# A causal zero block kept in tiles, the last outputs in pairs, and a swish written in token order by ScalarE

## The chip, the cores and the metric

The kernel runs on one core of a Trainium2 chip. A core has five engines that run beside each other and meet through semaphores: TensorE (matmuls; the profile calls it PE, and its weight loads PEld), VectorE (DVE), ScalarE (ACT), GpSimd (POOL) and SyncE (SP), which here issues DMAs. Matmuls write to PSUM, eight banks of 128 partitions by 512 floats; all else lives in SBUF or, between stages, in DRAM. The metric is the time of one execution on the device in microseconds; less is better. All data is float32. Where a matmul's operand is to be exact, it is split into a rounded part `hi` (type float32r) and a rest `lo`, and three products (hi·hi, hi·lo, lo·hi) replace one.

## The reference, cut to what matters

One layer of a decoder: `SEQ` 1024 tokens, `D_MODEL` 1024 channels. A mixing sub-layer runs a convolution branch and an attention branch on the same input; a SwiGLU sub-layer follows.

```
def hybrid_mixer(h, ...):
    proj = h @ w_in
    glu_in, qkv, gates = split(proj)
    u = u_val * sigmoid(u_gate)
    u = causal_depthwise_conv(u, conv_w, conv_b)          # 31 taps, 512 channels
    u = silu(layernorm(u, conv_ln_g, conv_ln_b))
    y_conv = u @ w_conv_out
    o = stick_breaking_attention(q, k, v)                 # 8 heads of 64
    y_att = o @ w_att_out
    merged = sigmoid(g_conv) * y_conv + sigmoid(g_att) * y_att
    return merged @ w_o

# stick-breaking attention, for each block of queries; causal means key < query
z = q k^T / 8
a = where(causal, exp(log_sigmoid(z) + sum of log_sigmoid(-z) over the later keys), 0)
o = a @ v

x = x + ga1 * rmsnorm(hybrid_mixer(h))
x = x + ga2 * rmsnorm((silu(gate) * up) @ w_ffn_out)      # gate, up = split(h2 @ w_ffn_in)
```

## The kernel before, in words

Channels lie on partitions and tokens in the free dimension, except in attention, where the scores have queries on partitions. Two mechanisms set the order of instructions. Most of the kernel is written in plain program order and is ordered by a planner (`TileContext(nc, schedule_with_timeline_sim=True)`): it takes what is ready on a simulated timeline, by priority; priority is the place in the program, and `tc.high_priority(offset=...)` moves a block forward. The engines' queues are then fixed, and each runs its own strictly in that order. Some stretches are ordered by hand: `pin(start)` (line 186) chains all instructions issued since `start` on TensorE, VectorE and ScalarE. A buffer is a tile of a pool with a `tag` and a number of `bufs`; a new tile of that tag waits for the readers of the one whose place it takes.

**Attention** (lines 522 to 598, function `head`, called eight times under high priority). For each pair of query blocks `c` (256 queries, four pairs in all; the order of the pairs is in `CORDER`) and each half of up to 512 keys, `z` comes from two matmuls (lines 551, 552) and, on the diagonal, a third that adds the mask (554). ScalarE takes two sigmoids of it (555, 556), VectorE a running product from right to left (559) and a product (561); the result `beta` has queries on partitions. For each pair of key blocks `jp`, TensorE turns four 128x128 blocks into one PSUM bank `tr` (line 571: two key blocks `jj` by two query blocks `ii`). ScalarE copies the bank to `ahi` (574), VectorE subtracts to get `alo` (575), both 128x512 with two buffers in turn, and four matmuls with the values add to `av` (580, 581). Where `jp == c`, the block with the later keys and the earlier queries is zero by causality; there the transpose reads the constant tile `zeros`. A head has ten such banks, four of them on the diagonal: 80 and 32 in all. The matmuls of projections, values, the input gate (`glu`), the convolution (`conv`) and the merge gates are written around the heads, and the planner places them between the steps of attention.

**The convolution's normalisation and swish** (`ln_all`, lines 724 to 762). The convolution works with tokens split by their remainder modulo eight (`PH = 8`), so its output `cacc[ct]` lies as eight runs of 128: `(r m)`, remainder first. The normalisation keeps that order. Then, for each of four channel tiles of 128x1024, ScalarE writes the sigmoid of the scaled input to `csig` (756) and the scaled input over itself (757); VectorE multiplies the two and writes to `csil` in token order `(m r)` (760), that is, with a step of eight floats between successive elements. `split_r` (718) makes `chi` and `clo` of it, which are the operands of the convolution branch's projection (`y_conv`, 774). `ln_all` is issued with `LN_PRI` ahead of the rest of the merge gates' last five products (`other_five`, 689), which use ScalarE and VectorE for their own splits (`w_op`, 399).

**The end** (lines 1673 to 1709). The last projection is done by quarters (a Strassen-Winograd scheme of seven products). The last quarter of tokens by channels, `c == 0`, runs in two halves of 256 tokens, `h = 0, 1`. In the second, the sums for the norm end on TensorE (`fsum`, 1708), `rstd_from` (150) makes the factor `rs`, and `finish` (1613) writes the outputs: for `m` of 0 to 3 and `i` of 0 to 1, a 128x256 product with `rs` (line 1626 for `m < 2`, line 1629 for the rest, which reads the result from PSUM, `last`), an addition of the residual `xr` (1631, through `add`, 1528), and a DMA of each pair to the output (1632, `load`, 103).

Of the kernel before, what the change touches and what calls it, by code (L numbers as in the profile page):

```python
# [11 lines left out]
F32R = mybir.dt.float32r  # L12
BF16 = mybir.dt.bfloat16
AF = mybir.ActivationFunctionType
# [61 lines left out]
def tile_block(ctx: ExitStack, tc: tile.TileContext, xT, vecs, ada1, ada2, win, wv, wcv, wat, wo, w1, w2, cvw, out):  # L76
# [341 lines left out]
    with ExitStack() as sC:  # L418
        pc = mkpool(sC, "pc")
        with ExitStack() as sA:  # L420
# [69 lines left out]
            def qk_pair(p):  # L490
# [28 lines left out]
                            dve.tensor_tensor(kl[i][dst, cs], b[c][src], ks[i][src, cs], op=ALU.subtract)  # L519
                return qs, ks, kl  # L520

            def head(p, hh, qst, kst, klo, vts, oT):
                half = slice(0, HD) if hh == 0 else slice(HD, P)
                other = slice(HD, P) if hh == 0 else slice(0, HD)
                hidx = (2 * p + hh) % 4
                tag = f"{p}_{hh}"
                av = None
                order = CORDER[2 * p + hh]
                for ci, c in enumerate(order):
                    if ci % 2 == 0:  # L530
                        av = psv.tile([P, CH], F32, tag="av", name=f"av{tag}_{c}")
                    avc = av[:, (c % 2) * 256:(c % 2) * 256 + 256]
                    kaps = {}
                    nsc = 1 if c < 2 else 2
                    for sc in range(nsc - 1, -1, -1):
                        probs = []
                        for i in (2 * c, 2 * c + 1):
                            W = P * (i + 1)
                            if i not in kaps:
                                kaps[i] = pa.tile([P, T], F32, tag="kap", name=f"ka{tag}_{i}", bufs=2)  # L540
                            kap = kaps[i]
                            s_lo, s_hi = sc * CH, min(W, (sc + 1) * CH)
                            w = s_hi - s_lo
                            beta = pa.tile([P, CH], F32, tag="beta", name=f"be{tag}_{i}_{sc}", bufs=4)
                            tcols = slice(i * P, (i + 1) * P)
                            z = psz.tile([P, CH], F32, tag="z", name=f"z{tag}_{i}_{sc}")
                            z_lo = s_lo if w >= 256 else max(0, s_hi - 256)
                            z_hi = max(s_hi, z_lo + 256)
                            zw, zo = z_hi - z_lo, s_lo - z_lo
                            diag = s_hi == W  # L550
                            pe.matmul(z[:, :zw], qst[:, tcols], kst[:, z_lo:z_hi], start=True, stop=False)  # L551
                            pe.matmul(z[:, :zw], qst[:, tcols], klo[:, z_lo:z_hi], start=False, stop=not diag)
                            if diag:
                                pe.matmul(z[:, zo + w - P:zo + w], identb, mask, start=False, stop=True)  # L554
                            act.activation(kap[:, s_lo:s_hi], z[:, zo:zo + w], AF.Sigmoid, bias=0.0, scale=-0.125)  # L555
                            act.activation(beta[:, :w], z[:, zo:zo + w], AF.Sigmoid, bias=0.0, scale=0.125)  # L556
                            rev = kap[:, s_lo:s_hi][:, ::-1]
                            init = 1.0 if diag else kap[:, s_hi:s_hi + 1]
                            dve.tensor_tensor_scan(rev, rev, rev, init, op0=ALU.mult, op1=ALU.bypass)  # L559
                            m = w - 1 if diag else w  # L560
                            dve.tensor_tensor(beta[:, :m], beta[:, :m], kap[:, s_lo + 1:s_lo + 1 + m], op=ALU.mult)  # L561
                            probs.append(beta)
                        for jp in range(min(c, 2 * sc + 1), 2 * sc - 1, -1):
                            tr = pst.tile([P, CH], F32, tag="tr", name=f"tr{tag}_{c}_{jp}")
                            for jj in range(2):
                                j = 2 * jp + jj
                                for ii in range(2):
                                    jo = (j - 4 * sc) * P
                                    src = zeros if (jp == c and jj == 1 and ii == 0) else probs[ii][:, jo:jo + P]
                                    o = jj * 256 + ii * P  # L570
                                    pe.transpose(tr[:, o:o + P], src, ident)  # L571
                            ahi = pa.tile([P, CH], F32R, tag="ahi", name=f"ahi{tag}_{c}_{jp}", bufs=2)
                            alo = pa.tile([P, CH], F32R, tag="alo", name=f"alo{tag}_{c}_{jp}", bufs=2)
                            act.activation(ahi, tr, AF.Copy)  # L574
                            dve.tensor_tensor(alo, tr, ahi, op=ALU.subtract)  # L575
                            for jj in range(2):
                                j = 2 * jp + jj
                                lhs = vts[j][:, hidx].rearrange("p a d -> p (a d)")
                                cols = slice(jj * 256, jj * 256 + 256)
                                pe.matmul(avc, lhs, ahi[:, cols], start=(jp == c and jj == 0), stop=False)  # L580
                                pe.matmul(avc, lhs, alo[:, cols], start=False, stop=(jp == 0 and jj == 1))  # L581
                    if ci % 2 == 1:
                        cs = slice((c // 2) * CH, (c // 2 + 1) * CH)
                        act.activation(oT[half, cs], av[other], AF.Copy)
                        dve.tensor_tensor(oT[half, cs], av[half], oT[half, cs], op=ALU.add)
# [47 lines left out]
    with ExitStack() as sG:  # L633
# [90 lines left out]
        def ln_all():  # L724
# [27 lines left out]
            for ct in range(CONVT):  # L752
                a = cacc[ct]
                g, b_ = vec[:, C_LNG + ct:C_LNG + ct + 1], vec[:, C_LNB + ct:C_LNB + ct + 1]
                sg = hp.tile([P, T], F32, tag="act", name=f"csig{ct}")
                act.activation(sg, a, AF.Sigmoid, bias=b_, scale=g)
                act.activation(a, a, AF.Identity, bias=b_, scale=g)
                o = hp.tile([P, T], F32, tag="act", name=f"csil{ct}")
                ar, sr = (t.rearrange("p (r m) -> p r m", r=PH) for t in (a, sg))
                (pool if ct in SILU_POOL else dve).tensor_tensor(  # L760
                    o.rearrange("p (m r) -> p r m", r=PH), ar, sr, op=ALU.mult)
                cacc[ct] = o

        a2 = deque(range(2 * KT, 4 * KT))
# [689 lines left out]
    with ExitStack() as sG:  # L1454
# [144 lines left out]
        def sq_tile(name):  # L1599
            return po_.tile([P, CH], F32, tag="wt", name=name, bufs=3)  # L1600
# [12 lines left out]
        def finish(c, h, ps_sum, yy, last=None):  # L1613
# [2 lines left out]
            dcols = slice(c * CH + h * n, c * CH + (h + 1) * n)  # L1616
            rs = pg.tile([P, CH], F32, tag="rs", name=f"frs{c}{h}", bufs=2)[:, :n]
            m, a = (sq_tile(f"frs{c}{h}{i}")[:, :n] for i in "ma")
            rstd_from(rs, m, a, ps_sum, D)
            for m in range(4):  # L1620
                xr = xrs[c, m]
                y = ytile[yy[m // 2], m % 2]
# [157 lines left out]
```

## Time and profile before

| | us |
|---|---|
| median of 3 runs | 1416.66 |
| lowest and highest | 1416.08, 1422.94 |
| profiled execution | 1420.87 |
| its span, first to last instruction | 1419.1 |
| TensorE busy in that span | 1389.1 |
| VectorE busy | 1061.3 |
| ScalarE busy | 650.8 |
| GpSimd busy | 96.3 |

The profile is one execution, 4.2 us above the median. Its views name an instruction by engine, line, operation and tile, with its form (partitions x elements, type); durations are in us on the timeline and in ns in groups. In the groups, the part behind the last bar is idle time of the engine just before these instructions, and what ended it. Matmuls overlap in their pipeline, so a matmul's duration is longer than the distance to the next one's start. A wait for several semaphores is put down to the one that came last.

### The profile page before, as it was taken

The numbers are of one execution on the slowest core, as the hardware profiler recorded it, in microseconds if no ns is written. First come the engines' busy times: TensorE is split into PE (matmuls) and PEld (weight loads), VectorE is DVE, ScalarE is ACT, GpSimd is POOL, SyncE is SP. The second block draws the span as 40 slices with busy tenths as digits, with TensorE's granted clock in tenths as the row PEclk, the third lists the DMA queues.
The fourth block names the chain that finished last, engine by engine and source line by source line (L and its number), as shares of the span: only waits on it lengthen the run. The fifth ranks groups of instructions, "written<-read, shape, count | busy, mean of one in ns | idle before, by whom it ended". The sixth has DMA issues, their size and how long they took to land.

```text
span 1419.1 us, 18807 instructions
## 1 busy us (share of the span) xinstructions
PE 1389.1 (98%) x6886; PEld 1161.1 (82%) x6886; DVE 1061.3 (75%) x1602; ACT 650.8 (46%) x1136; POOL 96.3 (7%) x183
## 2 busy tenths in 40 slices
PE   7999999999999999999999999999999999999996
PEld 4888898898888878888877778888888887888886
DVE  6788688666776779779589878788777776785357
ACT  5275466354553547413356543334444444433441
POOL 0000000000000101000011110001111110000000
PEclk8899999999999999999999999999999999999999
DMA  9112032122163654784934535456777769588733
GB/s 383 64 45 75 30 110 84 45 80 99 51 204 104 224 178 165 282 280 133 375 121 163 180 146 171 165 177 206 252 254 252 261 235 390 178 331 287 279 117 119
DMA packets 91116, 258.73 MB, mean 182 GB/s; under 512 B 9744, under 2 KB 20112, under 8 KB 90000
## 3 DMA queue, kind: packets, MB, share of 16 engines
q1 hardware_dynamic: 75088, 202.99, 42.0%
q0 software_dynamic: 15936, 54.54, 10.2%
q8 instruction: 54, 0.88, 0.3%
q14 instruction: 38, 0.31, 0.1%
HBM read 190.91 MB, written 66.58 MB: 181 GB/s over the span
## 4 chain that ended last, share of the span: by engine, by line
PE 87%; DVE 6%; DMA 3%; ACT 2%; issue 1%; SPq 0%; DVEq 0%; ACTq 0%; POOLq 0%
PE ka L958 12%; PE ka L1489 9%; PE kc L958 7%; PE pwo L881 6%; PE pb L1489 4%; PE pgv L180 3%; PE pg L180 3%; PE pyc L180 3%; PE pya L180 3%; PE pv L481 3%; PE pcv L461 3%; PE ka L415 2%; PE tr L571 2%; PE ke L1066 2%; PE pq L180 2%; PE pgg L180 2%
## 5 line engine op out<-in xcount | busy, mean ns | idle before, releaser
L559 DVE TENSOR_TENSOR_SCAN ka<-ka 128x128 f32<-128x128 f32 (+2 forms) x96 | 91.4, 968 | 22.8 <-ACT ka L555 22.5
L555 ACT ACTIVATE ka<-z 128x128 f32<-128x128 f32 (+2 forms) x96 | 47.1, 496 | 59.1 <-PE z L554 32.6
L575 DVE TENSOR_TENSOR alo<-tr,ahi 128x512 fp32r<-128x512 f32 x80 | 53.2, 685 | 18.2 <-ACT ahi L574 17.7
L574 ACT ACTIVATE ahi<-tr 128x512 fp32r<-128x512 f32 x80 | 46.4, 602 | 37.7 <-PE tr L571 25.9
L1489 PE MATMUL ka<-gt,w2f 128*128 128x512 f32 x264 | 63.4, 389 | 0.1
L561 DVE TENSOR_TENSOR be<-be,ka 128x127 f32<-128x127 f32 (+2 forms) x96 | 53.4, 572 | 9.7 <-ACT be L556 5.0
L1489 PEld LDWEIGHTS ka<-gt,w2f 128*128 128x128 f32 x264 | 49.5, 188 | 10.8 <-issue 0.5
L1066 PE MATMUL ke<-b,w_hi 128*128 128x512 f32 x176 | 55.1, 394 | 0.0
L135 DVE SCALAR_TENSOR_TENSOR ada<-ada,cb 128x1024 f32<-128x1024 f32 x32 | 38.8, 1223 | 19.6 <-DMA ada<-in_ada_dram 19.6
L556 ACT ACTIVATE be<-z 128x128 f32<-128x128 f32 (+2 forms) x96 | 46.2, 496 | 9.6 <-PE tr L571 9.5
L571 PE MATMUL tr<-ident,be 128*128 128x128 f32 x288 | 47.8, 273 | 0.4 <-DVE alo L575 0.4
L580 PE MATMUL av<-ahi,vst 128*128 128x256 f32 x160 | 44.2, 292 | 0.0
L461 PE MATMUL pcv<-ph,cvw 128*128 128x128 f32 x320 | 42.5, 276 | 0.9 <-DMA ph<-v_d 0.9
L581 PE MATMUL av<-alo,vst 128*128 128x256 f32 x160 | 42.8, 293 | 0.0
L461 PEld LDWEIGHTS pcv<-ph,cvw 128*128 128x128 f32 x320 | 39.5, 192 | 1.6 <-issue 1.3
L1066 PEld LDWEIGHTS ke<-b,w_hi 128*128 128x128 f32 x176 | 33.0, 188 | 7.8 <-issue 1.0
L481 PE MATMUL pv<-wv_hi,hhi 128*128 128x256 f32 x128 | 36.8, 288 | 2.1 <-DVE qst L505 1.4
L159 ACT ACTIVATE gt<-X 128x512 fp32r<-128x512 f32 x33 | 20.4, 630 | 39.1 <-PE ka L1489 12.1
L481 PE MATMUL pv<-wv_hi,hlo 128*128 128x256 f32 x128 | 36.7, 287 | 0.0
L481 PE MATMUL pv<-wv_lo,hhi 128*128 128x256 f32 x128 | 36.4, 285 | 0.0
L551 PE MATMUL z<-kst,qst 128*128 128x256 f32 (+2 forms) x96 | 36.2, 382 | 0.0
L571 PEld LDWEIGHTS tr<-ident,be 128*128 128x128 f32 x288 | 34.7, 140 | 1.8 <-PE z L554 0.5
(532 smaller groups left out, 4108.5 us busy)
## 6 DMA issues: line engine op xcount, KB each, us to landing
w_d<-w2o POOLq DMA_DIRECT2D x44, 512.0 KB, 8.1
w2f<-w_d SPq DMA_DIRECT2D x44, 512.0 KB, 4.9
ada<-in_ada_dram SPq DMA_DIRECT2D x32, 512.0 KB, 5.6
w2r<-in_w_dram SPq DMA_DIRECT2D x44, 256.0 KB, 4.0
w1g<-in_w_dram SPq DMA_DIRECT2D x21, 512.0 KB, 3.6
w1u<-in_w_dram SPq DMA_DIRECT2D x21, 512.0 KB, 4.8
cvw<-in_cvw_dram SPq DMA_DIRECT2D x20, 512.0 KB, 3.7
ada_w<-in_ada_dram SPq DMA_DIRECT2D x8, 1024.0 KB, 12.0
```

The lines of the kernel that those rows point to most:

```text
L180: pe.matmul(bank, st[:, cols], mv[k][:, c * CH:(c + 1) * CH], start=(i == 0 and s == 0), stop=(i == n - 1 and s == 2))
L461: pe.matmul(cv[:, gi * TM:(gi + 1) * TM], wts[n][:, at:at + P], ph[:, g, SH - 1 - d:SH - 1 - d + TM], start=(d == 0), stop=(d == SH - 1))
L481: pe.matmul(pv[:, :256], st[k][:, tcols], mv[:, wc], start=(k == 0 and i == 0), stop=(k == KT - 1 and i == 2))
L555: act.activation(kap[:, s_lo:s_hi], z[:, zo:zo + w], AF.Sigmoid, bias=0.0, scale=-0.125)
L559: dve.tensor_tensor_scan(rev, rev, rev, init, op0=ALU.mult, op1=ALU.bypass)
L561: dve.tensor_tensor(beta[:, :m], beta[:, :m], kap[:, s_lo + 1:s_lo + 1 + m], op=ALU.mult)
L571: pe.transpose(tr[:, o:o + P], src, ident)
L575: dve.tensor_tensor(alo, tr, ahi, op=ALU.subtract)
L881: pe.matmul(bank_, st[:, cols], mv[k][:, cs], start=(k == 0 and q == 0), stop=(k == KT - 1 and q == 2))
L958: pe.matmul(bank_, st[:, cols], t[:, mv], start=(first and j == 0 and s == 0), stop=(j == HK - 1 and s == 2), skip_group_check=not first)
L1066: pe.matmul(kbs[f], wes[f][st][:, cols], t[:, mv], start=(i == 0 and j == 0 and q == 0), stop=(j == HK - 1 and q == 2), skip_group_check=i ...
L1489: pe.matmul(dst, w[st][:, cols], g[mv], start=first and s == 0, stop=last and s == 2, skip_group_check=more)
```

## The change

There are three edits.

First, attention. Four tiles that live through all heads (two pairs of `ahi` and `alo`) get zeros in their first 128 columns once. On the diagonal (`on`), the two halves of the bank change places, three blocks are turned instead of four, and ScalarE and VectorE copy and subtract the last 384 columns into these tiles, taken in turn. Elsewhere all stays as it was, with the two rotating buffers for those banks alone. The matmuls with the values keep their number and size.

Second, the swish. ScalarE writes the sigmoid to `sg` and the scaled input to `o`, both in token order, from the remainder-first `a`; VectorE multiplies them in place with unit step.

Third, the end. In the call of `finish` with `last`, ScalarE copies three residual pairs (128x512) to PSUM banks ahead of `rstd_from`. Then GpSimd does the output pair 0 in two operations of 128x512 (`rs` repeated by a broadcast), VectorE does pairs 2 and 3 with two 128x256 scale steps and one 128x512 addition from PSUM each, and pair 1 with one product and one addition of 128x512. SP issues the DMAs in the order 2, 3, 0, 1. This stretch is pinned.

```diff
+            diag_t = []
+            for i in range(2):
+                t = [pa.tile([P, CH], F32R, name=f"{nm}d{i}") for nm in ("ahi", "alo")]
+                for x in t:
+                    dve.tensor_copy(x[:, :P], zeros)
+                diag_t.append(t)
+            ndiag = count()
...
+                            on = jp == c
                             for jj in range(2):
                                 j = 2 * jp + jj
                                 for ii in range(2):
+                                    if on and jj == 1 and ii == 0:
+                                        continue
                                     jo = (j - 4 * sc) * P
-                                    src = zeros if (jp == c and jj == 1 and ii == 0) else probs[ii][:, jo:jo + P]
-                                    o = jj * 256 + ii * P
-                                    pe.transpose(tr[:, o:o + P], src, ident)
-                            ahi = pa.tile([P, CH], F32R, tag="ahi", name=f"ahi{tag}_{c}_{jp}", bufs=2)
-                            alo = pa.tile([P, CH], F32R, tag="alo", name=f"alo{tag}_{c}_{jp}", bufs=2)
-                            act.activation(ahi, tr, AF.Copy)
-                            dve.tensor_tensor(alo, tr, ahi, op=ALU.subtract)
+                                    o = (jj ^ on) * 256 + ii * P
+                                    pe.transpose(tr[:, o:o + P], probs[ii][:, jo:jo + P], ident)
+                            if on:
+                                ahi, alo = diag_t[next(ndiag) % 2]
+                                used = slice(P, CH)
+                            else:
+                                ahi = pa.tile([P, CH], F32R, tag="ahi", name=f"ahi{tag}_{c}_{jp}", bufs=2)
+                                alo = pa.tile([P, CH], F32R, tag="alo", name=f"alo{tag}_{c}_{jp}", bufs=2)
+                                used = slice(0, CH)
+                            act.activation(ahi[:, used], tr[:, used], AF.Copy)
+                            dve.tensor_tensor(alo[:, used], tr[:, used], ahi[:, used], op=ALU.subtract)
...
-                cols = slice(jj * 256, jj * 256 + 256)
+                cols = slice((jj ^ on) * 256, (jj ^ on) * 256 + 256)
...
                 sg = hp.tile([P, T], F32, tag="act", name=f"csig{ct}")
-                act.activation(sg, a, AF.Sigmoid, bias=b_, scale=g)
-                act.activation(a, a, AF.Identity, bias=b_, scale=g)
                 o = hp.tile([P, T], F32, tag="act", name=f"csil{ct}")
-                ar, sr = (t.rearrange("p (r m) -> p r m", r=PH) for t in (a, sg))
-                (pool if ct in SILU_POOL else dve).tensor_tensor(
-                    o.rearrange("p (m r) -> p r m", r=PH), ar, sr, op=ALU.mult)
+                ar = a.rearrange("p (r m) -> p r m", r=PH)
+                act.activation(sg.rearrange("p (m r) -> p r m", r=PH), ar, AF.Sigmoid, bias=b_, scale=g)
+                act.activation(o.rearrange("p (m r) -> p r m", r=PH), ar, AF.Identity, bias=b_, scale=g)
+                dve.tensor_tensor(o, o, sg, op=ALU.mult)
...
+            if last:
+                xp = {}
+                for mm_ in (2, 3, 1):
+                    xp[mm_] = bank(f"x1p{mm_}").rearrange("p (a b) -> p a b", a=2)
+                    act.activation(xp[mm_], xrs[c, mm_][:, :, cols], AF.Copy)
             rstd_from(rs, m, a, ps_sum, D)
+            if last:
+                r2 = rs.unsqueeze(1).to_broadcast([P, 2, n])
+                y0, y1, y2_, y3 = (ytile[yy[m // 2], m % 2][:, :, cols] for m in range(4))
+
+                def put(m, y):
+                    load(out[2 * m:2 * m + 2, :, dcols].rearrange("n p t -> p n t"), y)
+
+                begin = len(nc.cur_bb.bb.instructions)
+                pool.tensor_tensor(y0, y0, r2, op=ALU.mult)
+                pool.tensor_tensor(y0, y0, xrs[c, 0][:, :, cols], op=ALU.add)
+                for m, y in ((2, y2_), (3, y3)):
+                    for i in range(2):
+                        dve.scalar_tensor_tensor(y[:, i], last[2 * (m - 2) + i][:, cols],
+                                                 gpost2[:, 2 * m + i:2 * m + i + 1], rs, op0=ALU.mult, op1=ALU.mult)
+                    add(dve, y, y, xp[m])
+                    put(m, y)
+                dve.tensor_tensor(y1, y1, r2, op=ALU.mult)
+                add(dve, y1, y1, xp[1])
+                put(0, y0)
+                put(1, y1)
+                pin(begin)
+                return
```

## The prediction, on record before the result

> **What bounds the kernel now.** I read the page first: totals, then the chain that ended last.
>
> ```profile
> PE 1389.1 (98%) x6886; PEld 1161.1 (82%) x6886; DVE 1061.3 (75%) x1602; ACT 650.8 (46%) x1136; POOL 96.3 (7%) x183
> PE 87%; DVE 6%; DMA 3%; ACT 2%; issue 1%; SPq 0%; DVEq 0%; ACTq 0%; POOLq 0%
> ```
>
> TensorE is the bound, but an average hides stages, so I asked for busy time by stretch: attention (80 to 440), the convolution's normalisation and swish (545 to 600), the last step (from 1408). Columns: length, then PE, PEld, DVE, ACT, POOL busy with counts, granted clock, DMA.
>
> ```profile
> 80.00:440.00 360.00, 358.07 (x2277) 316.27 (x2276) 262.68 (x372) 194.16 (x403) 7.12 (x7) 1.00 0.26 83
> 545.00:600.00 55.00, 54.80 (x239) 44.37 (x239) 47.10 (x61) 33.93 (x41) 5.40 (x10) 1.00 0.67 235
> 1408.00:1419.00 11.00, 0.00 (x0) 0.00 (x0) 6.96 (x19) 0.72 (x2) 0.00 (x0) 0.70 0.28 95
> ```
>
> The first two are TensorE's at full granted clock; in the last TensorE does nothing, and DVE and the output DMAs set the end. The view of waits says how often TensorE stood still in attention (total us, times, longest):
>
> ```profile
> PE pcv L461 <- DMA ph<-v_d: 0.9, 1, 0.9
> PE pv L481 <- DVE vst L486: 0.7, 1, 0.7
> PE tr L571 <- DVE alo L575: 0.4, 1, 0.4
> ```
>
> That is 2.0 us in 360. Attention's own chain (scores, scan, transpose, copies) has holes, but other matmuls fill them. So in attention a TensorE instruction saved is time saved; an ACT or DVE instruction saved there is worth at most those 2.0 us.
>
> **Zero block kept in tiles.** Removed: one transpose of `zeros` per head and query pair.
>
> ```profile
> L571 PE MATMUL tr<-ident,zeros x32: 270/272/279, 89.2 to 422.1; 128*128 128x128 f32 x32
> ```
>
> Its 272 ns are pipelined, so the price is the distance between starts:
>
> ```profile
> 89.14 0.27 PE L571 MATMUL tr<-ident,be 128*128 128x128 f32 x1
> 89.25 0.27 PE L571 MATMUL tr<-ident,zeros 128*128 128x128 f32 x1
> 89.36 0.27 PE L571 MATMUL tr<-ident,be 128*128 128x128 f32 x1
> ```
>
> 0.11 us each, 32 times: 3.5 us. The weight load beside it goes too, and its time is inside that distance.
>
> The 32 diagonal copies and subtractions shrink from 512 to 384 columns. Nearest rows by form:
>
> ```profile
> L574 ACT ACTIVATE ahi<-tr 128x512 fp32r<-128x512 f32 x80 | 46.4, 602 | 37.7 <-PE tr L571 25.9 <-PE av L580 11.2
> L555 ACT ACTIVATE ka<-z 128x384 f32<-128x384 f32 x16 | 8.0, 498 | 20.6 <-PE z L554 19.3 <-DVE be L561 1.1
> L575 DVE TENSOR_TENSOR alo<-tr,ahi 128x512 fp32r<-128x512 f32 x80 | 53.2, 685 | 18.2 <-ACT ahi L574 17.7
> L561 DVE TENSOR_TENSOR be<-be,ka 128x383 f32<-128x383 f32 x16 | 8.8, 549 | 0.8
> ```
>
> ACT saves 32 x 0.10 = 3.3 us and DVE 32 x 0.14 = 4.4 us, both beside TensorE; with four buffers in turn instead of two, ACT's 11.2 us of waiting for `av` shrink as well. I count all of it at nothing; the bound is the 2.0 us above.
>
> Added: four 128x128 copies of zeros on DVE. Nearest row, and the place where they fit:
>
> ```profile
> L254 DVE TENSOR_SCALAR dia<-ident,csil 128x128 f32<-128x128 f32 x8 | 1.7, 280 | 0.0
> 71.53 1.23 DVE L169 TENSOR_TENSOR wv_lo<-wv_raw,wv_hi 128x1024 fp32r<-128x1024 f32 x1 [10.21 <-PE pk L331]
> ```
>
> 4 x 0.28 = 1.1 us into a 10.2 us hole ahead of the first use: nothing. Put behind the hole they would delay the first `qst`, and TensorE by up to 1.1 us.
>
> **Swish.** DVE's product was written with a step of 8 floats (32 bytes) between elements; now ACT's sigmoid and identity are written so, and DVE multiplies unit-step in place.
>
> ```profile
> L756 ACT ACTIVATE csig<-cr,vec 128x1024 f32<-128x1024 f32 x4 | 5.0, 1240 | 1.0 <-DVE csil L760 1.0
> L760 DVE TENSOR_TENSOR csil<-cr,csig 128x1024 f32<-128x1024 f32 x4 | 8.8, 2188 | 0.0
> L721 DVE TENSOR_TENSOR clo<-csil,chi 128x1024 fp32r<-128x1024 f32 x4 | 5.0, 1238 | 0.0
> L443 DVE TENSOR_TENSOR u<-pgv,sg 128x512 f32<-128x512 f32 x8 | 8.1, 1082 | 1.6 <-PE pgv L180 1.6
> L783 DVE TENSOR_TENSOR yc<-pyc,yc 128x512 f32<-128x512 f32 x16 | 10.4, 684 | 0.0
> ```
>
> Stepped, DVE pays 2188 against 1238 ns, and in the convolution's input gate (L443) 1082 against 684 (L783): 0.8 to 0.9 ns an element more. So DVE saves 4 x 0.95 = 3.8 us. No ACT row has a stepped write. Bounds for its eight: nothing more (1240 stays), or DVE's surcharge, 8 x 0.95 = 7.6 us. I take the surcharge, an estimate from DVE's rows: inputs there were read in unit step, so the write is what cost, and it is the same memory. The Trainium skill (SBUF — State Buffer, section "Door 1: The DMA port swizzle") says that SBUF works in lines of 16 bytes, that consecutive accesses within a line go at full rate, and that each access to a new line pays. By that rule ACT pays too, which speaks against this edit; the trace agrees for DVE, and no run here shows ACT.
>
> What would it cost TensorE? The timeline of that stretch:
>
> ```profile
> 557.25 0.63 ACT L159 ACTIVATE s1o<-gs 128x512 fp32r<-128x512 f32 x1 [0.50 <-PE ka L415]
> 558.28 2.19 DVE L760 TENSOR_TENSOR csil<-cr,csig 128x1024 f32<-128x1024 f32 x1
> 559.45 0.62 ACT L159 ACTIVATE s2o<-gs 128x512 fp32r<-128x512 f32 x1
> 560.12 0.30 PEld L415 LDWEIGHTS ka<-T2o,s2o 128*128 128x128 f32 x2 [0.15 <-ACT s2o L159]
> 561.04 2.17 PEld L415 LDWEIGHTS kc<-T1o,s1o 128*128 128x128 f32 x10 [0.63 <-DVE s1o L402]
> 565.50 1.25 ACT L756 ACTIVATE csig<-cr,vec 128x1024 f32<-128x1024 f32 x1 [1.00 <-DVE csil L760]
> 569.82 1.04 ACT L159 ACTIVATE chi<-csil 128x1024 fp32r<-128x1024 f32 x1
> 573.91 0.84 PE L180 MATMUL pyc<-chi,wc_hi 128*128 128x512 f32 x3
> ```
>
> TensorE has no slack behind ACT at `s2o` (560.12 waits for it). Three of the eight writes stand before it in ACT's queue: 3 x 0.95 = 2.85, less the 0.50 that ACT idled at 557.25: 2.3 us late. Behind all eight, `chi` at 569.82 is later by 7.6 less 1.5 of idle time (0.50 and 1.00): ready at 577.0 and not 570.9, where TensorE wants it at 573.9: 3.1 us. The operands queued behind `chi` on DVE can stretch that to about 4.7. At the other end, with ACT unchanged, DVE's saving removes the waits of 0.15 and 0.63: 0.8 us won. I take 2.3 lost, the place with a wait already in the trace, since the planner may set the convolution's product a little later.
>
> **Last quarter.** Rows: DVE's last steps, eight 512-wide adds, POOL's only elementwise row, ACT's idle time before the end, the output DMA.
>
> ```profile
> 1409.84 1.43 DVE yc L1626 x4
> 1411.28 1.57 DVE yc L1629 x4
> 1412.76 2.76 DVE L1529 TENSOR_TENSOR yc<-yc,xr 128x256 f32<-128x256 f32 x8
> 1391.75 4.90 DVE L1529 TENSOR_TENSOR yc<-yc,xr 128x512 f32<-128x512 f32 x8
> L169 POOL TENSOR_TENSOR wv_lo<-wv_raw,wv_hi 128x1024 fp32r<-128x1024 f32 x2 | 5.5, 2761 | 47.0 <-ACT wv_hi L159 47.0
> 1402.20 0.38 ACT L1707 ACTIVATE fsq<-ka 128x256 f32<-128x256 f32 x1 [3.58 <-PE ka L1489]
> out_dram<-yc SPq DMA_DIRECT2D x8, 256.0 KB, 2.3
> ```
>
> From 1409.84 DVE works to 1412.76 + 2.76 = 1415.52: 5.7 us. After: four 256-wide scale steps (1.57), then three adds and one product of 512 columns at 4.90 / 8 = 0.61 each: 4.0 us. Saved 1.7; as most of them now read the instruction just before, I take 1.4. Block 0 goes to POOL: two operations of 512 columns at half of 2.76, 2.8 us, done by 1412.6, before DVE. POOL would have to be half as slow again to set the end; at double the row's price `y0` is ready at 1415.4 and the gain is 0.1 us. A PSUM operand costs DVE nothing: L575, which reads `tr` there, has 685 and L783 684. The three ACT copies into PSUM (no row; about 0.6 us each by L574, which goes the other way) fit into ACT's holes such as 3.58 us; left to the end they would add 1.8. The four output DMAs stay 256 KB, landing 2.3 us after issue; the last follows DVE's last add as now. On SP's queue the DMA of block 0 stands ahead of the last one, so a late POOL would hold that too.
>
> **Sum.** -3.5 (transposes) + 2.3 (swish) - 1.4 (end) = -2.6 us. The profiled execution took 1420.87 (span 1419.1), so 1418.3 in its terms; it lies 4.2 above the median of the runs, 1416.66, from which I forecast 1414.1. A measurement of this kernel tells about 0.5% (7.1 us) from no change.
>
> **Rivals.**
> *ACT's stepped writes are free.* For: ACT is another engine than the one whose rows show the surcharge. Against: the memory is the same. Then -3.5 - 0.8 - 1.4 = -5.7: 1411.0. Chance 0.26.
> *The transposes' time is not recovered.* The planner orders everything anew, and other waits take the 3.5 us. For: several queues there stand close together (waits of 0.4 to 0.9 us above). Against: 2.0 us of waiting in 360. 1417.6; chance 0.15.
> *Every cover gives way well.* Rival one, and attention's 2.0 us of TensorE waits vanish with the shorter copies: -7.7, 1409.0. Chance 0.12.
> *Slower: a convolution ahead of its data.* Each convolution waits for a round trip through memory:
>
> ```profile
> v_d<-u SPq DMA_DIRECT2D x4, 512.0 KB, 2.9
> ph<-v_d SPq DMA_DIRECT2D x4, 512.0 KB, 5.5
> ```
>
> That is 8.4 us, covered by filler matmuls but for the 0.9 us wait above. With less attention work to interleave, the new order could place a convolution's matmuls before the data. Two of four uncovered give 1414.1 + 16.8 = 1430.9; slower by over 0.5% begins at 9.6 us lost, a little over one. Against: the planner orders by a simulated timeline that has the DMAs in it, and in the order of now one convolution of four waits, for 0.9 us. Chance 0.10.
>
> **How the numbers follow.** The forecast has 0.37. The range runs from 1408, just under the third rival with the end at its bound (1409.0 less 0.3), to 1420: the second rival with the swish at its upper price, 1417.6 + 2.4. The slower rival and a little of both tails stay out, under 0.2. Faster by over 0.5% means below 1409.6: the third rival and a quarter of the first, 0.18. Slower means above 1423.7: the last, 0.10. Same: 0.72.
>
> **What would show it.** Right: L571's zeros gone, 288 transposes left; diagonal copies of 128x384 near 0.5 us; `csig` and `csil` on ACT near 2.1 us; the in-place product near 1.24; TensorE waiting for ACT near 560 or 574; from the last `frs` to the last add 4.0 to 4.3 us, with POOL done before. Wrong: ACT's writes at 1.24 (first rival); new waits in attention's list (second); `pcv` waiting for `ph` by several us (the slower one); the last DMA held by POOL's `y0`.

## The result and the profile after

| | before | after |
|---|---|---|
| median of the runs, us | 1417.04 (6 runs, 1415.04 to 1422.94) | 1426.7 (6 runs, 1425.11 to 1428.21) |
| ratio to before | | 1.0058, 95% interval 1.0041 to 1.0075 |
| profiled execution, its span | 1420.87, 1419.1 | 1426.41, 1424.6 |

The change makes the kernel slower by 0.58%, 9.7 us. The forecast was 1414.1 us with a range of 1408 to 1420: the time lies above the range, and on the other side of the kernel before. The totals of the page after look as planned: TensorE has 32 instructions fewer and is busy for 3.9 us less, and DVE for 7.2 us less.

```profile
PE 1385.2 (97%) x6854; PEld 1157.4 (81%) x6854; DVE 1054.1 (74%) x1598; ACT 658.4 (46%) x1139; POOL 98.5 (7%) x185
```

So the 9.7 us are time in which TensorE waited or ran slowly. The waits of TensorE from 440 to 780 us, first the kernel before, then the kernel after (total us, times, longest):

```profile
PE ka L415 <- DVE gv L703: 1.2, 1, 1.2
PE ka L415 <- ACT s2o L159: 0.3, 1, 0.3
PE kc L415 <- DVE s1o L402: 0.2, 1, 0.2
```

```profile
PE pwo L895 <- DVE sga L835: 4.7, 1, 4.7
PE kc L415 <- ACT s1o L159: 2.7, 1, 2.7
PE ka L415 <- DVE gw L722: 2.2, 2, 2.0
```

1.7 us have become 9.6. The rest is behind these waits, in the granted clock. The busy time by stretch of the kernel after (length, PE, PEld, DVE, ACT, POOL with counts, clock, DMA share, GB/s), each stretch laid on one piece of the clock's record:

```profile
553.38:556.80 3.42, 1.23 (x6) 0.69 (x4) 1.83 (x2) 3.42 (x3) 0.00 (x0) 1.00 0.81 280
556.80:560.21 3.41, 2.94 (x7) 2.32 (x8) 2.67 (x4) 3.41 (x3) 0.00 (x0) 0.51 0.98 381
570.50:573.91 3.41, 3.41 (x10) 2.63 (x9) 3.41 (x5) 3.41 (x6) 0.54 (x1) 0.50 0.63 244
672.90:679.72 6.82, 6.11 (x14) 4.79 (x15) 4.13 (x5) 1.06 (x1) 0.00 (x0) 0.50 0.73 232
679.72:686.00 6.28, 6.28 (x29) 5.19 (x28) 0.00 (x0) 0.00 (x0) 0.00 (x0) 1.00 1.00 342
```

Read the clock column against the waits: TensorE idles for 2.7 us until 557.3, and from 556.8 the clock is 0.5 for 3.41 us; so it is from 570.5, behind the 2.0 us that ended at 569.1, and from 672.9 for 6.82 us, around the end of the 4.7 us (673.6). In the last stretch but one 14 matmuls run, in the next, a little shorter, 29. The kernel before has the clock at 1.00 in all of this part. So a wait here costs its own length and then half of 3.41 or 6.82 us of TensorE's work. The Trainium skill (TensorE: Matmul & The Clock Gate, section "🔬 Part 1: The HAM clock gate (the "warmup" mystery)") says that the clock follows TensorE's activity in free-running windows of 3413 ns; the lengths here agree. The Trainium skill (TensorE: Matmul & The Clock Gate, section "HAM oscillation — how this bites in real kernels") gives idle gaps above some 3.4 us as the ones to avoid; here 2.0 us did it, and the measurement decides.

The table puts the difference into stages, between the starts of named matmuls: attention (first `pv` to last `k`), merge gates and convolution branch (to last `pyc`), output projection (last `pya` to first `ke`), everything from there to the last `fsum`, and the end. The stretch from `pyc` to the last `pya` is 43.52 us in every kernel. "Whole" runs from the first `pv` to the last instruction. I leave out the start: its half-clock stretch lasts 20.48 us in the profile before and 10.24 in the one after, the first `pv` comes at 74.3 and 70.0 us, and these 4.4 us blur any comparison of spans. The first row is in us, the others are differences to it.

| kernel | attention | gates, conv. | output proj. | to `fsum` | end | whole |
|---|---|---|---|---|---|---|
| before | 422.30 | 128.90 | 89.36 | 649.06 | 11.61 | 1344.75 |
| after | -3.58 | +7.42 | +7.85 | -0.93 | -0.82 | +9.93 |
| zero block alone | -3.22 | +1.81 | +6.69 | -0.09 | -0.01 | +5.18 |
| swish alone | -0.01 | +9.11 | 0.00 | -1.31 | -0.01 | +7.78 |
| end alone | -0.11 | +0.09 | +0.33 | -0.31 | -0.82 | -0.82 |
| zero block, end, bank moved | -3.71 | +2.52 | +0.68 | -0.46 | -0.83 | -1.80 |
| the same, second time | -3.60 | +1.64 | -0.01 | -0.77 | -0.82 | -3.56 |
| all three edits, bank moved | -3.57 | +7.22 | +0.45 | -1.26 | -0.83 | +2.01 |

The whole of the kernel after (+9.93) agrees with the difference of the medians (9.7). The part "to `fsum`" scatters by about 1 us with no edit in it, also in the two traces of one kernel; less than that is not read from this table.

The boundary between the first two columns moves with the zero block. In every kernel that has it, five `ka` matmuls stand ahead of the last `k` and not twelve; the other seven, 7 x 0.227 = 1.6 us of work, have passed from the attention column into the next. The lines at the last `k`, first before, then after:

```profile
496.63 0.39 PE L415 MATMUL k<-hhi,a 128*128 128x512 f32 x1
496.85 2.88 PE L415 MATMUL kc<-T1o,s1o 128*128 128x512 f32 x12
```

```profile
488.68 0.39 PE L415 MATMUL k<-hhi,a 128*128 128x512 f32 x1
488.91 1.75 PE L415 MATMUL ka<-T2o,s2o 128*128 128x512 f32 x7
```

So the two columns have to be added: from the first `pv` to the last `pyc` the zero block gains 1.4 us alone, and 1.2 and 2.0 us in the two traces of the kernel with zero block, end and moved bank, whose end edit does nothing there (-0.02 alone).

### The profile page after: what moved, and what is told of

Its sections match the earlier page's. It is cut to its first block, busy times and chain, and to the rows that moved or that the text cites. A ratio compares the mean times of both kernels' runs of the same rounds, so it can differ in the third digit from the quotient of the medians.

```text
span 1424.6 us, 18700 instructions
## 1 busy us (share of the span) xinstructions
PE 1385.2 (97%) x6854; PEld 1157.4 (81%) x6854; DVE 1054.1 (74%) x1598; ACT 658.4 (46%) x1139; POOL 98.5 (7%) x185
## 4 chain that ended last, share of the span: by engine, by line
PE 76%; issue 10%; DVE 6%; DMA 4%; ACT 2%; POOL 1%; SPq 0%; POOLq 0%; DVEq 0%; ACTq 0%
PE ka L972 14%; PE ka L1503 9%; PE kc L972 8%; PE pwo L895 6%; PE pb L1503 4%; PE pgv L180 3%; PE pg L180 3%; PE pv L481 3%; PE ke L1080 2%; PE pgg L180 2%; PE pk L180 2%; PE pcv L461 2%; PE pa L1503 2%; PE kb L972 2%; PE tr L581 2%
## 5 line engine op out<-in xcount | busy, mean ns | idle before, releaser
L895 PE MATMUL pwo<-mhi,wo_hi 128*128 128x512 f32 x88 | 35.8, 409 | 4.7 <-DVE sga L835 4.7
L519 DVE TENSOR_TENSOR klo<-pk,kst 64x512 fp32r<-64x512 f32 x32 | 22.0, 689 | 22.9 <-ACT kst L516 22.5
L590 DVE TENSOR_TENSOR alo<-tr,ahi 128x512 fp32r<-128x512 f32 x48 | 32.3, 684 | 7.7 <-ACT ahi L589 7.4
L589 ACT ACTIVATE ahi<-tr 128x512 fp32r<-128x512 f32 x48 | 28.1, 602 | 17.4 <-PE tr L581 11.9
```

Of the source, the lines that this page charges most:

```text
L895: pe.matmul(bank_, st[:, cols], mv[k][:, cs], start=(k == 0 and q == 0), stop=(k == KT - 1 and q == 2))
```

## The experiments

My theory after the two traces took the 3.6 us of the attention column for the zero block's gain; two losses of more than 7 us each stand against it. One is ScalarE, whose stepped writes make it late for `s1o` and `gw`. The other has nothing to do with what the edits compute: the planner, with less attention work to place, hands out the PSUM banks in another order, and the last bank of the attention projection is now the one that the output projection needs first. The memory assignment of the two programs shows it:

```
          before   after
pya7_1    bank 2   bank 0
pwo0_0    bank 0   bank 0
```

The rivals: one of the two losses makes both waits; or the zero block's gain was never there, whatever stands behind it. From the timeline of the kernel after at that place (lines between these are left out):

```profile
668.03 0.69 DVE L835 TENSOR_TENSOR sga<-pya,sga 128x512 f32<-128x512 f32 x1
668.63 1.29 DVE L836 TENSOR_TENSOR yc<-yc,sga 128x512 f32<-128x512 f32 x2
669.96 1.06 ACT L159 ACTIVATE mhi<-yc 128x1024 fp32r<-128x1024 f32 x1 [3.09 <-DVE yc L836]
671.04 1.23 DVE L736 TENSOR_TENSOR mlo<-yc,mhi 128x1024 fp32r<-128x1024 f32 x1 [1.12 <-ACT mhi L159]
672.19 1.28 DVE L835 TENSOR_TENSOR sga<-pya,sga 128x512 f32<-128x512 f32 x2
673.61 0.77 PE L895 MATMUL pwo<-mhi,wo_hi 128*128 128x512 f32 x1 [4.71 <-DVE sga L835]
```

The readers of `pya7` stand in DVE's queue behind `mlo`, which waits for ScalarE's `mhi`. In the kernel before, the same order stands in DVE's queue, and TensorE passes it by: its first `pwo` goes to a bank that is free and starts at 669.27 us, ahead of these readers:

```profile
671.84 1.28 DVE L821 TENSOR_TENSOR sga<-pya,sga 128x512 f32<-128x512 f32 x2
```

### One edit at a time

Three kernels, each the kernel before with one of the three edits of the diff and nothing else. The first has the attention edit:

> Only the zero block kept in tiles. Theory: its 32 transposes give back 3.5 us on TensorE, but its new plan gives the last bank of the attention projection (pya7, second half) and the first bank of the output projection (pwo0_0) the same PSUM bank 0; before they were banks 2 and 0. TensorE then waits about 4.7 us for VectorE's last product from that bank and runs some 6.8 us at half clock after it (2.6 us more): -3.5 + 7.4 = about +4 us, ratio near 1.003, and no wait of TensorE for ScalarE in the swish. Rival: the wait at the output projection is the swish's delay handed on; then it is absent here and the ratio is near 0.9975.

Measured: 1421.88 us (1420.61 to 1425.39), ratio 1.003 [1.002, 1.0041]. Its two banks are the same as in the kernel after. The attention column is 3.2 us shorter, 1.6 of it the seven `ka`, and the kernel is slower. Its waits of TensorE from 440 to 780:

```profile
PE pwo L896 <- DVE sga L836: 3.7, 1, 3.7
PE ka L415 <- DVE gw L722: 1.1, 2, 0.8
PE pyc L180 <- ACT wc_hi L159: 1.1, 1, 1.1
```

The second has the swish:

> Only the swish edit. Theory: ScalarE's eight writes with a step of 32 bytes take about 2.3 us instead of 1.24, TensorE waits twice for some 2 to 3 us (s1o, then gw) and the granted clock is halved for 3.4 us after each: +7 to +8 us, ratio near 1.0055, and no wait at the first matmul of the output projection (its bank 0 is not the last one in use). Rival: the swish alone costs only the lag of 2.3 us that was forecast and the two long waits come from the new order of the zero block: ratio near 1.0015.

Measured: 1428.05 us (1424.15 to 1430.58), ratio 1.0067 [1.0047, 1.0086].

```profile
PE kc L415 <- ACT s1o L159: 5.3, 1, 5.3
PE ka L415 <- DVE gv L703: 1.2, 1, 1.2
```

One long wait of 5.3 us, where two of 2 to 3 us were expected, behind it 6.83 us of half clock, and no wait at `pwo` (its `pya7_1` is in bank 2). The profiled execution is the fastest of the six, 1424.15 us, so the table's 7.8 us are less than the loss by the medians. The swish alone costs more than in the kernel after; the planner orders the instructions around it otherwise there, and what of that makes the difference is not shown.

The third has the end:

> Only the pairs at the end. Theory: VectorE's part shortens from 5.7 to 4.4 us, the last output lands 1.5 us sooner after the last matmul, and the program ends 0.8 to 1.5 us sooner; ratio near 0.9992, too small to tell by time, so the trace decides. Rival: the two GpSimd operations or the DMA order give it back and the distance from the last fsum matmul to the end stays 11.6 us.

Measured: 1417.09 us (1414.55 to 1420.05), ratio 0.9993 [0.998, 1.0006], too little to tell from no change by the time; by the trace the end is 0.82 us shorter.

What follows: both losses come each with its own edit, and neither needs the other.

### The bank moved, without the swish

The zero block and the end, with `pya7_1` taken from another PSUM pool:

```diff
-            yb = {c: bkg(f"pya{n}_{c}") for c in range(NCH)}
+            yb = {c: bkg(f"pya{n}_{c}") if (n, c) != (7, 1) else psg.tile([P, CH], F32, tag="m", name="pya7_1")
+                  for c in range(NCH)}
```

> Zero block and pairs at the end, the swish as before, and one allocation changed: the last bank of the attention projection is taken from the other PSUM pool (bank 5), so that the output projection's first bank has long been free. Theory: no wait at the output projection, clock at full there; -3.5 for the transposes and about -1 for the end: 1412.5, ratio near 0.9968. Rival (the transposes' time is taken by other waits, or the last product is late whatever the bank): ratio 0.999 or more.

Measured: 1413.94 us (1412.73 to 1420.1), ratio 0.9972 [0.9959, 0.9986], faster than both kernels. `pwo` starts 0.23 us after the last `pya`, as in the kernel before, and the clock stays at 1.00. By the table it is 7.0 and 8.7 us shorter than the zero block alone, of which the end has 0.8.

### The bank moved, with all three edits

> The changed kernel whole, with one tile moved: pya7_1, the last PSUM bank of the attention projection, comes from another pool and takes bank 5 in place of bank 0, which pwo0_0 needs next. Theory: the bank cost the changed kernel 7.4 us (a wait of 4.7 us on sga and 2.6 us of half clock behind it) and the swish 7.9 us, and the two add. So this kernel loses the swish alone: about 1426.7 - 7.4 = 1419.3, between 1418 and 1421; pwo starts 0.2 us after the last pya and no half clock follows there; the ACT waits at s1o and gw near 556 and 570 stay. Rival: TensorE waits for something else at the output projection all the same (sga's other users), or the swish alone made all of the loss: above 1424.

Measured: 1420.89 us (1419.26 to 1423.02), ratio 1.0021 [1.0012, 1.0031]: 5.8 us under the kernel after by the medians, 7.4 by the table's column of the output projection. TensorE, VectorE and ScalarE run the same instructions in the same order as in the kernel after, so only the bank differs. What is left is the swish, in the column before it:

```profile
PE kc L415 <- ACT s1o L159: 2.6, 1, 2.6
PE ka L415 <- DVE gw L722: 1.5, 1, 1.5
```

In this trace the clock halves once, for 3.41 us behind the wait of 2.6 us, and not behind the 1.5 us.

### Is it the write, or any step?

The kernel just told, but ScalarE reads with the step (512 bytes) and writes in unit step:

```diff
-                ar = a.rearrange("p (r m) -> p r m", r=PH)
-                act.activation(sg.rearrange("p (m r) -> p r m", r=PH), ar, AF.Sigmoid, bias=b_, scale=g)
-                act.activation(o.rearrange("p (m r) -> p r m", r=PH), ar, AF.Identity, bias=b_, scale=g)
+                ar = a.rearrange("p (r m) -> p m r", r=PH)
+                act.activation(sg.rearrange("p (m r) -> p m r", r=PH), ar, AF.Sigmoid, bias=b_, scale=g)
+                act.activation(o.rearrange("p (m r) -> p m r", r=PH), ar, AF.Identity, bias=b_, scale=g)
```

> As the run with the bank moved, but ScalarE reads its input with the step (128 floats, 512 bytes) and writes sigmoid and identity in unit step, in the same token order; the product stays in place and unit-step on DVE. Theory A: a step costs ACT on whichever side it is, since each element touches another 16-byte line: csig and csil stay at about 2.3 us and the time at about 1419 to 1421. Theory B: only ACT's stepped write costs: csig and csil at 1.24 us, the waits at s1o and gw gone, and the time about 7 us lower, 1411 to 1413, below the run that has the old swish, by the 3.8 us that DVE saves if anything waits for it.

Measured: 1422.16 us (1419.21 to 1427.04), ratio 1.0036 [1.0023, 1.0049]. The groups of the kernel after, from 540 to 610 us, and of this one:

```profile
L773 ACT ACTIVATE csig<-cr,vec 128x1024 f32<-128x1024 f32 x4 | 9.2, 2312 | 0.0
L774 ACT ACTIVATE csil<-cr,vec 128x1024 f32<-128x1024 f32 x4 | 9.2, 2301 | 0.0
L775 DVE TENSOR_TENSOR csil<-csil,csig 128x1024 f32<-128x1024 f32 x4 | 4.9, 1226 | 4.9 <-ACT csil L774 4.9
```

```profile
L773 ACT ACTIVATE csig<-cr,vec 128x1024 f32<-128x1024 f32 x4 | 8.9, 2230 | 0.0
L774 ACT ACTIVATE csil<-cr,vec 128x1024 f32<-128x1024 f32 x4 | 8.8, 2208 | 0.0
```

The stepped read costs ScalarE as much as the stepped write, but for 0.1 us.

The other engine: zero block, end and moved bank with the old swish, in which DVE now reads both factors with the step and writes in unit step:

```diff
-                ar, sr = (t.rearrange("p (r m) -> p r m", r=PH) for t in (a, sg))
+                ar, sr = (t.rearrange("p (r m) -> p m r", r=PH) for t in (a, sg))
...
-                    o.rearrange("p (m r) -> p r m", r=PH), ar, sr, op=ALU.mult)
+                    o.rearrange("p (m r) -> p m r", r=PH), ar, sr, op=ALU.mult)
```

> The zero block, the new end and the moved bank with the swish of the kernel before, except that DVE's product reads both factors with a step of 512 bytes and writes in unit step, where it read in unit step and wrote with a step of 32 bytes. Theory A: a step costs DVE on either side, and two stepped inputs cost at least as much as one stepped output: csil at 2.2 us or more, the time at 1414 or above. Theory B: only the stepped write costs: csil near 1.24 us and the time at 1413 to 1414, at most 1 us below the kernel that it is made from, since TensorE waits for this step by 0.8 us in all in the kernel before.

Measured: 1417.97 us (1415.33 to 1422.48), ratio 0.9996 [0.9984, 1.0008].

```profile
L775 DVE TENSOR_TENSOR csil<-cr,csig 128x1024 f32<-128x1024 f32 x4 | 10.0, 2503 | 0.0
```

2503 ns, against 2188 with one stepped output and 1238 with none. So in all four places tried the reordering costs about 1 us or more per instruction of 128x1024: 0.95 as an output of DVE, 1.27 as its two inputs, 1.07 as an output of ScalarE and about 1.0 as its input. The kernel before had the cheapest of them (4 x 0.95 us), and the change bought it with two instructions per channel tile on ScalarE (8 x 1.07).

### Half of the swish

Zero block, end and moved bank, with the new swish for channel tiles 2 and 3 alone (`if ct >= 2:` before the three new instructions, the old ones otherwise), beside the same kernel with the old swish:

> The same kernel with the new swish for channel tiles 2 and 3 only; tiles 0 and 1 keep the old one. Theory: ACT's lag is a sum over its writes. The writes in front of s1o and s2o belong to tiles 0 and 1, so TensorE's wait of 2.7 us at s1o and the half clock behind it are gone, while four writes of 1.0 us more stand before the last chi and wc_hi: a wait of 1 to 3 us there or at gw, and a loss between none and all of the whole swish's: 1415 to 1419. Rival: the loss is not ACT's queue but something that every channel tile brings alike (the product in place, the buffers): half of the whole swish's 4 to 7 us, with waits at s1o as well.

> Zero block, new end and moved bank with the old swish, once more, as the base of the two other kernels of this job on the same chip: 1413.9, within 1413 to 1416; the two others are read against it.

Measured: half the swish 1415.65 us (1414.52 to 1422.09), ratio 0.9994 [0.9981, 1.0007]; none of it 1413.68 us (1412.85 to 1417.05), ratio 0.9977 [0.9967, 0.9988]. With half, the waits are:

```profile
PE ka L415 <- DVE gw L722: 1.7, 1, 1.7
PE pyc L180 <- ACT wc_hi L159: 1.0, 1, 1.0
PE pyc L180 <- DVE wc_lo L169: 0.7, 1, 0.7
```

No wait at `s1o`, no stretch of half clock, and a loss of 2.0 us by the medians, where the whole swish loses 7 (1420.89 less 1413.94). This fits a lag of ScalarE that is, at a place, the sum of the writes in front of it, and whose cost jumps when the wait grows long enough for the clock. The planner also moves a few instructions of ScalarE and DVE with the new swish; no run parts that from the longer writes.

### Matmuls in the gap

To part the idle time at `pwo` from the half clock behind it: the kernel after, with 20 needless matmuls into a bank that nobody waits for (the work added is no part of the result).

```diff
+            if n == KT - 1:
+                spare = psg.tile([P, CH], F32, tag="m", name="spare")
+                for i in range(20):
+                    pe.matmul(spare, ohi[0][:, :P], ohi[0][:, :CH], start=i == 0, stop=i == 19)
```

> The changed kernel with 20 needless matmuls of 128x512 (into a PSUM bank that nobody waits for) between the last matmul of the attention projection and the first of the output projection: 20 x 0.227 = 4.5 us of work in the idle stretch of 4.7 to 5.1 us that the shared bank makes. Theory: the first pwo still starts about 5 us after the last pya, as the wait on bank 0 is not touched, but the idle time is gone, so the half clock behind it goes too: pwo at 0.227 us from the start, and the time lower by 2.6 us, about 1424. Rival: the half clock comes from something else than the idle time (the change of stage, power): it stays, and the time is 1426.7 as before; if the matmuls only delay, it is higher still.

Measured: 1424.68 us (1423.22 to 1426.03), ratio 1.0048 [1.0035, 1.006], 2.0 us under the kernel after by the medians; the two intervals overlap, so the trace decides. From the timeline, and the stretch behind the gap:

```profile
670.52 4.70 PE L834 MATMUL spare<-ohi 128*128 128x512 f32 x20
675.23 0.47 PE L899 MATMUL pwo<-mhi,wo_hi 128*128 128x512 f32 x1
```

```profile
675.20:682.00 6.80, 6.79 (x31) 5.64 (x31) 3.44 (x4) 1.06 (x1) 0.00 (x0) 1.00 0.82 252
```

`pwo` starts nearly as late as in the kernel after, 4.9 us behind the start of the last `pya` and not 5.1; the clock is 1.00, and from the first `pwo` to the first `ke` 89.2 us pass and not 92.1. So the idle time makes the half clock, and of the bank's 7.85 us 4.9 are the wait and 2.9 the clock. In this one trace the whole is hardly shorter all the same (+9.66), since the convolution's stage took 1.9 us more, in which further waits of TensorE on DVE near 529 and 536 us stand; their cause is open.

### The end without POOL

By the trace POOL was done at 1419.0 in the kernel after, ahead of DVE; the last output landed at 1422.85; but the program ended 1.79 us after that landing, in the kernel before 1.08. POOL's sequencer has a drain in its record, from 1417.74 to 1423.87. To test it, the kernel with zero block, end and moved bank, with the two operations on DVE, ahead of the others:

```diff
-                pool.tensor_tensor(y0, y0, r2, op=ALU.mult)
-                pool.tensor_tensor(y0, y0, xrs[c, 0][:, :, cols], op=ALU.add)
+                dve.tensor_tensor(y0, y0, r2, op=ALU.mult)
+                dve.tensor_tensor(y0, y0, xrs[c, 0][:, :, cols], op=ALU.add)
+                put(0, y0)
```

> The kernel with zero block, new end, moved bank and old swish, except that block 0's two operations of the end are on DVE, at the end's beginning, and not on POOL. Theory: POOL's work, though done before DVE's, sets the program's end by what its queue does after its last operation; without it the program ends 1.08 us after the last output DMA has landed, as in the kernel before, and not 1.80. DVE has two steps of about 0.6 us more, so its last add comes 1.2 us later: from the last matmul to the end 10.8 - 0.7 + 1.2 = 11.3 us, and the time 0.5 us higher, 1413.9 to 1415. Rival: the 1.80 us comes from the paired DMAs or the three ACT copies; then it stays 1.8 and the end takes 12.0 us.

Measured: 1414.98 us (1413.69 to 1419.39), ratio 0.9986 [0.9975, 0.9998].

```profile
1402.93 0.69 DVE L1649 TENSOR_TENSOR yc<-yc,frs 128x512 f32<-128x512 f32 x1
1403.65 0.69 DVE L1650 TENSOR_TENSOR yc<-yc,xr 128x512 f32<-128x512 f32 x1
...
1408.00 0.69 DVE L1545 TENSOR_TENSOR yc<-yc,x1p 128x512 f32<-128x512 f32 x1
```

The last output landed at 1410.85 and the program ended at 1411.93, 1.08 us later; from the last `fsum` to the end 11.38 us pass, 0.6 more than with POOL. So POOL's two operations, with the drain behind them, took 0.7 us of the end's gain. By the trace POOL still pays for itself; by the times (1414.98 against 1413.68, intervals that overlap) that cannot be told.

## Why the prediction was wrong

**Transposes: the work right, the gain by luck.** 288 are left, the diagonal copies take 498 and 548 ns (0.10 and 0.14 less, as taken), and the time that TensorE spends on `tr`, from each start to the next matmul's, falls by 3.2 us. That attention is 3.6 us shorter, next to the -3.5 of the sum, is a coincidence: the seven `ka` took 1.6 us out of the stage, and other time in it grew by 1.2 us, 0.8 of this in TensorE's waits. Up to the last `pyc` only 1.2 to 2.0 us are gained. The second rival's sign, new waits in attention's list, was there: the wait for `ph` was 0.9 us before.

```profile
L581 PE MATMUL tr<-ident,be 128*128 128x128 f32 x288 | 47.4, 273 | 0.6 <-DVE be L569 0.6
L589 ACT ACTIVATE ahid<-tr 128x384 fp32r<-128x384 f32 x32 | 15.9, 498 | 12.9 <-PE tr L581 11.3 <-PE av L595 1.4
L590 DVE TENSOR_TENSOR alod<-tr,ahid 128x384 fp32r<-128x384 f32 x32 | 17.6, 548 | 4.2 <-ACT ahid L589 4.0
PE pcv L461 <- DMA ph<-v_d: 1.5, 1, 1.5
```

**What the new order does elsewhere: the step that failed first.** The sum priced the zero block at its own stage and nothing behind it. The second rival said that other waits could take the 3.5 us through the planner, and stopped there, at no gain. The zero block alone is in fact 5.2 us slower from attention on: 1.4 us gained up to the last `pyc`, and 6.7 us lost at the output projection (7.85 in the kernel after, 4.9 of waiting and 2.9 of half clock), where a bank is shared. The slower rival looked for the planner's mishap at `ph`; TensorE's wait there is 1.5 us in the kernel after. The mechanism was another: not a transfer placed too late, but the allocation of PSUM.

**Swish: the mechanism right, the term mis-sized.** ScalarE does pay, by 1.07 us an instruction and not 0.95, and TensorE waits near 557 and 569 us, about where it was said, in a profile whose attention starts 4.4 us earlier. The term was 2.3 with a bound of 4.7. In its stage the whole swish costs 4.7 to 5.6 us beside the zero block (+7.22 less 1.64 to 2.52) and 9.1 alone; by the medians it costs 7 beside the zero block. Two things were not in the term. I counted ScalarE's lag at one place, `s2o`, and took the later one at `chi` as an alternative; TensorE paid at `s1o` (2.7 us) and again at `gw` (2.0 us), through VectorE, which waited for ScalarE's part of `a`:

```profile
567.73 0.69 DVE L402 TENSOR_TENSOR a<-gw5b,a 128x512 fp32r<-128x512 f32 x1 [1.81 <-ACT a L159]
569.08 4.31 PE L415 MATMUL ka<-T4o,a 128*128 128x512 f32 x12 [1.99 <-DVE gw L722]
```

And I priced a wait of TensorE at its length. In the kernel after, the clock halved for 3.41 us behind each of the two, at about 1.7 us each. The Trainium skill's rule (SBUF — State Buffer, section "Door 1: The DMA port swizzle"), by which each access to a new 16-byte line pays, agrees with ScalarE's rows as well, for reads at a step of 512 bytes too (2230 ns against 1240).

**End: smaller.** From the last of `frs` to the last add DVE takes 4.43 us, and not 4.0 to 4.3:

```profile
1416.24 0.88 DVE L1651 SCALAR_TENSOR_TENSOR yc<-ka,gpost,frs 128x256 f32<-128x256 f32 x2
1416.43 1.26 POOL L1647 TENSOR_TENSOR yc<-yc,frs 128x512 f32<-128x512 f32 x1 [218.68 <-DVE frs L155]
1417.77 1.26 POOL L1648 TENSOR_TENSOR yc<-yc,xr 128x512 f32<-128x512 f32 x1
...
1419.98 0.69 DVE L1543 TENSOR_TENSOR yc<-yc,x1p 128x512 f32<-128x512 f32 x1
```

POOL took 1.26 us for each, less than the 1.4 of half the row, and was done first, as said. The gain was 0.82 us and not 1.4: DVE gave 1.26, the last output lands 1.5 us sooner after the last matmul, and POOL's drain took 0.7 back. That a PSUM operand costs DVE nothing had been read from two rows that both have one, L575 and L783; it holds here all the same, with 0.69 us for the adds of `x1p` from PSUM and 0.69 for that of `xr` from SBUF in the kernel without POOL.

**The sum again.** From the first `pv` to the last `pyc` +3.8, which is -1.2 to -2.0 for the zero block and +5.0 to +5.8 for the swish; then +7.85 (bank), -0.8 (end), -0.9 (scatter of the rest) = +9.9.

## What to carry to other kernels

Where a planner orders the work and hands out buffers, a small edit is also a new plan: after it, look at the waits of the bound engine over the whole program, and at whether two neighbouring stages share a PSUM bank, before judging the edit by the time. In these traces an idle stretch of TensorE of 2 us or more could cost its length and half of 3.4 or 6.8 us behind it, so a lag is to be priced with the clock. A change of layout cost about 1 us or more per 128x1024 instruction on both engines, whether they read or wrote with the step: leave it where the fewest instructions carry it.

## What the hardware did that I had not expected

- In each trace the changes of the clock lie on one grid of 3.41 us, and what counted was TensorE's idle time inside one window of this grid. From the first `pv` to 1395 us, over all traces, each of the nine full-clock windows with 1.92 us of idle time or more (1.92 to 3.41) was followed by half clock, and none with 1.59 us or less was. So idle times of nearly one length went two ways: the 1.99 us of the kernel after lay in one window (first line), the 2.11 us of the kernel with DVE's stepped reads in two, 1.04 and 1.07 us of it (second and third line).

```profile
567.08:570.49 3.41, 1.42 (x7) 1.19 (x7) 1.86 (x3) 3.41 (x4) 0.54 (x1) 1.00 0.48 141
561.03:564.44 3.41, 2.37 (x11) 1.63 (x9) 3.41 (x4) 3.13 (x3) 0.00 (x0) 1.00 1.03 419
564.44:567.86 3.42, 2.35 (x10) 1.98 (x11) 3.42 (x4) 1.80 (x4) 0.54 (x1) 1.00 1.02 419
```

- The half clock lasted a second window, 6.83 us in all, where TensorE idled for 0.72 us or more of the first (0.72, 1.09, 1.10), behind idle times of 3.7, 4.7 and 5.3 us; it lasted one where it idled for 0.43 us or less.
- A stepped operand costs ScalarE 1.07 us per 128x1024 when written at 32 bytes (2312 against 1240 ns) and about 1.0 when read at 512 bytes (2230). DVE takes 2503 ns with two inputs stepped at 512 bytes and 2188 with its output stepped at 32 bytes, against 1238 with unit step.
- In the kernel after, the drain in POOL's queue lasted until 6.1 us after the start of POOL's last elementwise operation, 4.8 us behind that operation's end.
